# Which units of a transformer layer's second feed-forward product use seven block products, and when their sums are combined

## The chip, the cores and the metric

One core of one Trainium2 chip. The metric is the device time of one execution in microseconds (us), as the median of several runs; single executions that were profiled have a span, from the first to the last instruction, beside it.

## The reference

One decoder layer with 256 tokens of width 1024 in fp32: two groups of attention heads, an output projection, a normalisation, a SwiGLU feed-forward part of inner width 2816, and a second normalisation. The part that the change touches is the last:

```
gu = jnp.einsum('bsd,df->bsf', x, w_ffn_in[l])
g, u = jnp.split(gu, 2, axis=-1)
f = jnp.einsum('bsf,fd->bsd', jax.nn.silu(g) * u, w_ffn_out[l])
x = layer_norm(ALPHA * x + f, ln2_g[l], ln2_b[l])
```

## The kernel before

Every fp32 matrix product is made of three matmuls in a rounded format: an operand is split into a high part (`hi`, a rounding copy on ScalarE) and the rest (`lo`, a subtraction on VectorE), and hi x hi, hi x lo and lo x hi are summed in PSUM. Weights come in units of 128 x 4 x 512 numbers (1 MB). Each is loaded by SyncE's queue into one of the four `raw` buffers of the pool `wraw`, split into one of four `hi` and one of four `lo` buffers, and multiplied.

The inner width 2816 is worked in 11 chunks of 256. The first product (`ffn_rows` for chunks 0 and 1, `ffn_cols` for chunks 2 to 10) needs two weight units per chunk and writes the gated result of chunk c into `hTh[c]` and `hTl[c]`. The second product (from line 650) needs one weight unit per chunk, U0 + v for v = 0 to 10. For a chunk, the output of 256 tokens x 1024 columns is a 2 x 2 matrix of blocks (token tile t of 128, column half n of 512), the inner width gives a 2 x 2 matrix of factors, so a plain unit needs eight block products of three matmuls, 24 in all, which go to the PSUM banks c11, c12, c21 and c22.

For the chunks in `SEVEN` the same blocks come from seven products (Winograd's scheme), 21 matmuls: of the sums T0 to T3 of weight blocks and sums of blocks of h. Products 1, 5, 6 and 7 go to banks of their own and are shared by several output blocks; the other three go to c11, c12 and c21. `ffn_cols` makes the sums of h (lines 615 to 625, tile `hq`), and `split_seven` (line 687) the sums of weights: T in a tile `t` that takes another of the four `raw` buffers, and three of the T split into `th` and `tl` of the pool `tq`, which has two buffers of each. `tq` is opened at line 652, after the pools `hq` and `rpool2` of the first product have been closed at line 646. `load_unit` loads a unit of `SEVEN` in three pieces.

`ahead2(v, 2)` loads up to three units ahead of v and splits up to two ahead. The loop at line 719 multiplies units 0 to 7 (`TAIL` is 8), in the order c11, c12, c21, c22, 1, 6, 5, 7 of each unit. The last three units, 8, 9 and 10, of which 8 and 10 are in `SEVEN`, are multiplied bank by bank from line 735: all three units' products for bank 1, then c11, 6, 5, c12, 7, c22, and behind each of them the operations that add that bank to the output `z` (with alpha times the residual `x1`), each on VectorE but for two copies on ScalarE. The products for c21 come last, in two halves of 256 columns with PSUM tiles of their own (`fo_tail`). `ln_stats` takes the mean and variance (`bn_aggr`, line 510) and a power on GpSimd (line 512); `center` (line 774) and `finish` (line 778) normalise, and each finished piece is stored. The order on each engine is a list that is fixed when the kernel is built; it follows the order in the source where operands are expected to be ready, and takes later work forward where they are not.

Of the kernel before, what the change touches and what calls it, by code (L numbers as in the profile page):

```python
# [11 lines left out]
F32 = mybir.dt.float32  # L12
# [3 lines left out]
ALU = mybir.AluOpType  # L16

P = 128
S = 256
D = 1024  # L20
# [3 lines left out]
NCH = DFF // 256  # L24
# [3 lines left out]
ALPHA = 2.0 ** 0.25  # L28
# [12 lines left out]

SEVEN = (2, 4, 6, 8, 10)


SWAP = [(i + HALF) % 16 if i < 16 else i for i in range(32)]
# [9 lines left out]
def hybrid_layer_kernel(ctx, tc, xT, xr, w_in, w_o, w_f1, w_f2, cols, rows, lamb, rot, tri, out):  # L57
    nc = tc.nc

    const = ctx.enter_context(tc.tile_pool(name="const", bufs=1))  # L60
    wraw = ctx.enter_context(tc.tile_pool(name="wraw", bufs=4))
# [20 lines left out]
    raw, hi, lo = {}, {}, {}  # L82
    state = {"load": 0, "split": 0}

    def load_unit(u, pieces=1):
        t = wraw.tile([P, 4, 512], F32, tag="raw", name=f"raw{u}")
        if u - (NU - NCH) in SEVEN:

            for a, b, w in ((3, 1, 1), (0, 0, 1), (1, 2, 2)):
                nc.sync.dma_start(t[:, a : a + w, :], units[u][:, b : b + w, :])  # L90
            raw[u] = t
            return
        n = 4 // pieces
        for i in range(pieces):
            nc.sync.dma_start(t[:, i * n : (i + 1) * n, :], units[u][:, i * n : (i + 1) * n, :])
        raw[u] = t
# [14 lines left out]
    def split_unit(u, pieces=1):  # L111
        for _ in split_gen(u, pieces):
            pass
# [373 lines left out]
    x1 = lnp.tile([P, 2, D], F32, name="x1")  # L487
    z = mpool.tile([P, 2, D], F32, name="z")
# [8 lines left out]
    st = {}  # L497
# [8 lines left out]
    def ln_stats(name, t):  # L506
        mv = small.tile([P, 2], F32, tag="mv", name=f"mv{name}{t}")
        rs = small.tile([P, 1], F32, tag="rs", name=f"rs{name}{t}")
        n = 4 if (name, t) == ("f", 1) else 2
        nc.vector.bn_aggr(mv, st[name, t][:, :n, :].rearrange("p a b -> p (a b)"))  # L510
        nc.vector.tensor_scalar(rs, mv[:, 1:2], EPS, None, op0=ALU.add)  # L511
        nc.gpsimd.tensor_tensor(rs, rs, mhalf[:, :1], op=ALU.pow)  # L512
        return mv, rs
# [44 lines left out]
    for c in range(NCH):  # L558
        shape = [P, 7, P] if c in SEVEN else [P, 2, S]
        hTh[c] = hp.tile(shape, F32R, name=f"hTh{c}")  # L560
# [33 lines left out]
    def ffn_cols(c, j):  # L594
# [13 lines left out]
        nc.scalar.activation(gate, gate, AF.Silu)  # L608
        if c not in SEVEN:
            nc.vector.tensor_mul(up, up, gate)  # L610
# [40 lines left out]
    TAIL = NCH - 3  # L651
# [5 lines left out]
    bank = {}  # L657
# [6 lines left out]
    def prods(v):  # L664

        u = U0 + v
        H, L = hTh[v], hTl[v]
        W = lambda i: (hi[u][:, i, :], lo[u][:, i, :])
        if v not in SEVEN:
            A = lambda t, kk: (H[:, kk, t * P : (t + 1) * P], L[:, kk, t * P : (t + 1) * P])  # L670
            return {f"c{t + 1}{n + 1}": [(A(t, kk), W(2 * kk + n)) for kk in range(2)]
                    for t in range(2) for n in range(2)}
        A = lambda i: (H[:, i, :], L[:, i, :])
        T = lambda i: (TH[v][:, i, :], TL[v][:, i, :])
        return {"1": [(A(0), W(0))], "c11": [(A(1), W(1))], "6": [(A(5), T(1))], "5": [(A(4), W(3))],
                "c12": [(A(3), W(2))], "7": [(A(6), T(0))], "c21": [(A(2), T(2))]}

    def fo(name, v, last, ps=None, cs=slice(0, 512)):
        todo = prods(v).get(name, ())
        for m, ((ah, al), (wh, wl)) in enumerate(todo):  # L680
            key = name if ps is None else ps.name
            for i, (x, w) in enumerate(((ah, wh), (ah, wl), (al, wh))):
                nc.tensor.matmul(bank[name] if ps is None else ps, x, w[:, cs], start=key not in opened,  # L683
                                 stop=last and (m, i) == (len(todo) - 1, 2))
                opened.add(key)
# [20 lines left out]
    def ahead2(v, splits):  # L706
        u = U0 + v
        while state["load"] <= min(u + 3, NU - 1):
            load_unit(state["load"])
            state["load"] += 1  # L710
        while state["split"] <= min(u + splits, NU - 1):
            n = state["split"]
            state["split"] += 1
            if n - U0 in SEVEN:
                split_seven(n - U0)
            else:
                split_unit(n, 1)

    for v in range(TAIL):
        ahead2(v, 2)  # L720
        for name in ("c11", "c12", "c21", "c22", "1", "6", "5", "7"):
            fo(name, v, (name, v) == ("c21", TAIL - 1))
    ahead2(TAIL, 2)
    tail = range(TAIL, NCH)

    zt = lambda t, n: z[:, t, 512 * n : 512 * n + 512]
    xt = lambda t, n: x1[:, t, 512 * n : 512 * n + 512]
    z = wraw.tile([P, 2, D], F32, tag="raw", name="z2")
    s156 = wraw.tile([P, 3, 512], F32, tag="raw", name="s156")
    s1, s5, s6 = (s156[:, i, :] for i in range(3))  # L730
    st["f", 0] = small.tile([P, 4, 6], F32, tag="st", name="stf0")
    st["f", 1] = small.tile([P, 4, 6], F32, tag="st", name="stf1")

    nc.vector.scalar_tensor_tensor(zt(1, 0), xt(1, 0), ALPHA, bank["c21"], op0=ALU.mult, op1=ALU.add)
    for name in ("1", "c11", "6", "5", "c12", "7", "c22"):
        for v in tail:
            fo(name, v, not any(name in prods(w) for w in tail if w > v))
        if name == "1":
            nc.scalar.copy(s1, bank["1"])
            nc.vector.scalar_tensor_tensor(zt(0, 0), xt(0, 0), ALPHA, s1, op0=ALU.mult, op1=ALU.add)  # L740
        elif name == "c11":
            nc.vector.tensor_add(zt(0, 0), zt(0, 0), bank["c11"])
            nc.vector.bn_stats(st["f", 0][:, 0, :], zt(0, 0))
        elif name == "6":
            nc.vector.tensor_add(s6, s1, bank["6"])
            nc.vector.scalar_tensor_tensor(zt(0, 1), xt(0, 1), ALPHA, s6, op0=ALU.mult, op1=ALU.subtract)
        elif name == "5":
            nc.scalar.copy(s5, bank["5"])
            nc.vector.tensor_add(zt(0, 1), zt(0, 1), s5)
        elif name == "c12":  # L750
            nc.vector.tensor_add(zt(0, 1), zt(0, 1), bank["c12"])
            nc.vector.bn_stats(st["f", 0][:, 1, :], zt(0, 1))
        elif name == "7":
            nc.vector.tensor_add(s6, s6, bank["7"])
            nc.vector.tensor_add(zt(1, 0), zt(1, 0), s6)
            nc.vector.scalar_tensor_tensor(zt(1, 1), xt(1, 1), ALPHA, s6, op0=ALU.mult, op1=ALU.subtract)
            nc.vector.tensor_add(zt(1, 1), zt(1, 1), s5)
        else:
            nc.vector.tensor_add(zt(1, 1), zt(1, 1), bank["c22"])
            for j in range(2):  # L760
                nc.vector.bn_stats(st["f", 1][:, 2 + j, :], z[:, 1, 512 + 256 * j : 768 + 256 * j])

    for t in range(2):
        if t == 1:
            for j in range(2):
                cs, zs = slice(256 * j, 256 * j + 256), slice(256 * j, 256 * j + 256)
                ps = psB.tile([P, 256], F32, tag="b", name=f"fo_tail{j}")
                for v in tail:
                    fo("c21", v, v == NCH - 1, ps, cs)
                nc.vector.tensor_add(z[:, t, zs], z[:, t, zs], ps)  # L770
                nc.vector.bn_stats(st["f", t][:, j, :], z[:, t, zs])
        mv, rs = ln_stats("f", t)
        def center(a, b):
            nc.vector.scalar_tensor_tensor(z[:, t, a:b], z[:, t, a:b], mv[:, 0:1], rows2[:, 0, a:b],
                                           op0=ALU.subtract, op1=ALU.mult)

        def finish(a, b):
            nc.vector.scalar_tensor_tensor(z[:, t, a:b], z[:, t, a:b], rs, rows2[:, 1, a:b], op0=ALU.mult, op1=ALU.add)
            store(a, b)

        def store(a, b):
            nc.sync.dma_start(out[t * P : (t + 1) * P, a:b], z[:, t, a:b])

        if t == 0:
            for n in range(2):
                center(512 * n, 512 * n + 512)
                finish(512 * n, 512 * n + 512)
        else:
            center(512, 1024)
            finish(512, 1024)  # L790
            center(0, 512)
            finish(0, 256)
            finish(256, 512)


# [49 lines left out]
```

## Time and profile before

| | us |
|---|---|
| median of 3 runs | 318.17 |
| lowest and highest run | 318.13, 320.09 |
| profiled execution, its own time | 317.75 |
| its span | 315.8 |
| TensorE busy in the span | 300.4 |
| VectorE busy in the span | 254.3 |
| ScalarE busy in the span | 177.7 |

A profile's timeline gives for each instruction its start in us from the span's start, its length, its engine (PE is TensorE, DVE VectorE, ACT ScalarE, POOL GpSimd, SPq the queue of SyncE), its line, what it writes and reads, and in brackets how long the engine was idle before it and what released it. Consecutive instructions of an engine overlap by some hundredths to a tenth of a us. Matmuls are pipelined: their starts are 0.23 us apart where their lengths read 0.39.

### The profile page before, as it was taken

Reading aid. Unit: us, or ns where it says so; the run is one execution under the profiler, and the core shown is the slowest. Engines: PE = TensorE matmul, PEld = TensorE weight load, DVE = VectorE, ACT = ScalarE, POOL = GpSimd, SP = SyncE. Lnnn points to the kernel's source line nnn. Section 1 sums busy time; section 2 is a strip of 40 time slices with the busy share of each in tenths; the row PEclk is TensorE's granted clock in tenths of the full one; section 3 lists DMA queues with packets and bytes.
Section 4 is the critical chain, followed back from the end, with each engine's and each line's share of the span. In section 5 each row is a group of like instructions: output and inputs, shape, how many; then the busy total and the mean of one; then the engine's idle time right before and its main releaser. Section 6 shows DMA issues by size and latency. Waiting matters only on the chain.

```text
span 315.8 us, 4704 instructions
## 1 busy us (share of the span) xinstructions
PE 300.4 (95%) x1720; PEld 255.6 (81%) x1720; DVE 254.3 (81%) x476; ACT 177.7 (56%) x347; POOL 36.3 (11%) x38
## 2 busy tenths in 40 slices
PE   8899899999999999999999999999999999999960
PEld 5799789867887788888888888888888887888850
DVE  3799999999977289949397598578679779989595
ACT  3857479398685328247377457656664565654000
POOL 1076553310030010100000000000000000000011
PEclk9999999999999999999999999999999999999996
DMA  6989943333376432558654664474362436630002
GB/s 176 391 282 352 413 151 135 133 136 137 141 251 211 195 133 66 222 247 301 230 157 146 230 221 151 162 268 162 126 246 66 175 103 227 236 127 0 0 33 100
DMA packets 13749, 57.17 MB, mean 181 GB/s; under 512 B 1664, under 2 KB 2432, under 8 KB 8864
## 3 DMA queue, kind: packets, MB, share of 16 engines
q1 hardware_dynamic: 13440, 54.79, 49.8%
q0 software_dynamic: 288, 2.10, 1.8%
q8 instruction: 13, 0.21, 0.3%
q14 instruction: 8, 0.07, 0.1%
HBM read 55.84 MB, written 1.05 MB: 180 GB/s over the span
## 4 chain that ended last, share of the span: by engine, by line
PE 74%; DVE 15%; DMA 4%; issue 3%; POOL 1%; ACT 1%; SPq 1%; DVEq 0%; ACTq 0%
PE fc L601 21%; PE foc L683 13%; PE fc L602 11%; DVE lo L108 4%; PE fo L683 4%; DMA raw<-in_w_in_dram 4%; PE wo L142 2%; PE fr L143 2%; PE fr L142 2%; PE wo L144 2%; PE wo L143 2%; PE fr L144 2%; PE pj L142 2%; PE pj L144 2%; PE pj L143 2%
## 5 line engine op out<-in xcount | busy, mean ns | idle before, releaser
L108 DVE TENSOR_TENSOR lo<-raw,hi 128x512 fp32r<-128x512 f32 (+2 forms) x108 | 105.6, 1001 | 20.9 <-ACT hi L106 20.8
L106 ACT CAST hi<-raw 128x512 fp32r<-128x512 f32 (+2 forms) x116 | 90.2, 827 | 22.5 <-PE wo L144 9.9
L601 PE MATMUL fc<-x1T,hi 128*128 128x512 f32 x288 | 100.1, 392 | 0.0
L602 PE MATMUL fc<-x1T,lo 128*128 128x256 f32 x288 | 80.5, 280 | 0.0
L601 PEld LDWEIGHTS fc<-x1T,hi 128*128 128x128 f32 x288 | 54.1, 188 | 11.9
L602 PEld LDWEIGHTS fc<-x1T,lo 128*128 128x128 f32 x288 | 54.0, 188 | 0.0
L142 PE MATMUL pj<-xTh,hi 128*128 128x256 f32 x128 | 36.7, 294 | 1.4 <-ACT hi L190 1.4
L144 PE MATMUL pj<-xTh,lo 128*128 128x256 f32 x128 | 35.7, 286 | 0.6 <-DVE lo L108 0.5
L143 PE MATMUL pj<-xTl,hi 128*128 128x256 f32 x128 | 36.1, 284 | 0.0
L604 ACT COPY v<-fc 128x256 f32<-128x256 f32 x36 | 13.3, 370 | 27.6 <-PE fc L602 27.6
L142 PEld LDWEIGHTS pj<-xTh,hi 128*128 128x128 f32 x128 | 24.3, 192 | 3.0 <-ACT hi L190 2.5
L144 PEld LDWEIGHTS pj<-xTh,lo 128*128 128x128 f32 x128 | 24.1, 191 | 1.3 <-DVE lo L108 0.7
L143 PEld LDWEIGHTS pj<-xTl,hi 128*128 128x128 f32 x128 | 24.5, 191 | 0.0
L605 DVE TENSOR_TENSOR v<-v,fc 128x256 f32<-128x256 f32 x36 | 15.0, 418 | 11.3 <-ACT v L604 11.2
L512 POOL TENSOR_TENSOR rsf<-rsf,mhalf 128x1 f32<-128x1 f32 x2 | 1.8, 922 | 178.6 <-DVE rsf L511 178.6
L683 PE MATMUL foc<-hi,hTl 128*128 128x512 f32 x56 | 22.1, 395 | 0.0
L683 PE MATMUL foc<-lo,hTh 128*128 128x512 f32 x56 | 22.1, 394 | 0.0
L683 PE MATMUL foc<-hi,hTh 128*128 128x512 f32 x56 | 22.1, 394 | 0.0
L108 POOL TENSOR_TENSOR lo<-raw,hi 128x512 fp32r<-128x512 f32 x8 | 13.8, 1723 | 20.1 <-ACT hi L106 20.1
L284 ACT ACTIVATE E<-E,negm 128x128 f32<-128x128 f32 (+1 forms) x32 | 14.2, 444 | 2.5 <-DVE negm L281 2.4
L247 POOL TENSOR_TENSOR sh<-sh,cs_sb 128x256 f32<-128x256 f32 (+1 forms) x12 | 13.3, 1120 | 18.2 <-DVE sh L245 17.5
L142 PE MATMUL pj<-hi,xTh 128*128 128x512 f32 x32 | 13.7, 429 | 0.0
(201 smaller groups left out, 547.5 us busy)
## 6 DMA issues: line engine op xcount, KB each, us to landing
raw<-in_w_f_dram SPq DMA_DIRECT2D x28, 1024.0 KB, 5.1
raw<-in_w_in_dram SPq DMA_DIRECT2D x24, 256.0 KB, 5.5
raw<-in_w_in_dram SPq DMA_DIRECT2D x4, 1024.0 KB, 6.3
raw<-in_w_o_dram SPq DMA_DIRECT2D x4, 1024.0 KB, 4.8
raw<-in_w_f_dram SPq DMA_DIRECT2D x10, 256.0 KB, 3.5
raw<-in_w_f_dram SPq DMA_DIRECT2D x5, 512.0 KB, 4.6
raw<-in_w_in_dram SPq DMA_DIRECT2D x4, 512.0 KB, 8.4
rows<-in_rows_dram POOLq DMA_DIRECT2D x2, 1024.0 KB, 6.6
```

The lines of the kernel that those rows point to most:

```text
L106: nc.scalar.copy(h[:, s, :], r[:, s, :])
L108: eng.tensor_sub(l[:, s, :], r[:, s, :], h[:, s, :].bitcast(F32))
L142: nc.tensor.matmul(ps, sh, mh, start=first, stop=False)
L143: nc.tensor.matmul(ps, sh, ml, start=False, stop=False)
L144: nc.tensor.matmul(ps, sl, mh, start=False, stop=last)
L247: nc.gpsimd.tensor_mul(sh, sh, sin2[:, :m, :])
L284: nc.scalar.activation(e, e, AF.Exp, bias=negm[g][:, i, u : u + 1], scale=-1.0, accum_out=ls[g][:, i, u : u + 1])
L601: nc.tensor.matmul(ps, hi[u][:, i, ws], x1T[:, k], start=k == 0, stop=False)
L602: nc.tensor.matmul(ps[:, 0, :], lo[u][:, i, ws], x1T[:, k, 0, :], start=False, stop=k == KT - 1)
L604: nc.scalar.copy(v, ps[:, 1, :])
L605: nc.vector.tensor_add(v, v, ps[:, 0, :])
L683: nc.tensor.matmul(bank[name] if ps is None else ps, x, w[:, cs], start=key not in opened, stop=last and (m, i) == (len(todo) - 1, 2))
```

## The change

`SEVEN` becomes 2, 3, 4, 6 and 7, so that units 8, 9 and 10 are all plain. Within a unit the order of the products becomes 1, c11, 5, c12, 6, 7, c21, c22. Banks 1, 5, 6 and 7 are complete after unit 7; `combine`, which stands in the source behind all splits and ahead of the last three units' products, adds them and alpha times `x1` into `z`. The last three units then go to c11, c12 and c21, each followed by one sum into `z` and its statistics, and c22 comes last, in two halves of 256 columns. Tile 1 is finished in the order of its columns.

```diff
-SEVEN = (2, 4, 6, 8, 10)
+SEVEN = (2, 3, 4, 6, 7)
...
+    def combine():
+
+        uw = wraw.tile([P, 3, 512], F32, tag="raw", name="uw")
+        nc.scalar.copy(uw[:, 2, :], bank["1"])
+        nc.vector.scalar_tensor_tensor(zt(0, 0), xt(0, 0), ALPHA, bank["1"], op0=ALU.mult, op1=ALU.add)
+        nc.vector.tensor_add(uw[:, 0, :], uw[:, 2, :], bank["6"])
+        for t in range(2):
+            nc.vector.scalar_tensor_tensor(zt(t, 1), xt(t, 1), ALPHA, bank["5"], op0=ALU.mult, op1=ALU.add)
+        nc.vector.tensor_add(uw[:, 1, :], uw[:, 0, :], bank["7"])
+        nc.vector.tensor_sub(z[:, :, 512:], z[:, :, 512:], uw[:, 0:2, :])
+        nc.vector.scalar_tensor_tensor(zt(1, 0), xt(1, 0), ALPHA, uw[:, 1, :], op0=ALU.mult, op1=ALU.add)
+
     for v in range(TAIL):
         ahead2(v, 2)
-        for name in ("c11", "c12", "c21", "c22", "1", "6", "5", "7"):
-            fo(name, v, (name, v) == ("c21", TAIL - 1))
-    ahead2(TAIL, 2)
+        for name in ("1", "c11", "5", "c12", "6", "7", "c21", "c22"):
+            fo(name, v, name in ("1", "5", "6", "7", "c22") and not any(w in SEVEN or name == "c22" for w in range(v + 1, TAIL) if (w in SEVEN) != (name == "c22")))
+    z = wraw.tile([P, 2, D], F32, tag="raw", name="z2")
+    for v in range(TAIL, NCH):
+        ahead2(v, 2)
+    combine()
     tail = range(TAIL, NCH)
...
-    nc.vector.scalar_tensor_tensor(zt(1, 0), xt(1, 0), ALPHA, bank["c21"], op0=ALU.mult, op1=ALU.add)
-    for name in ("1", "c11", "6", "5", "c12", "7", "c22"):
-        for v in tail:
-            fo(name, v, not any(name in prods(w) for w in tail if w > v))
...
+    nc.vector.tensor_add(zt(1, 1), zt(1, 1), bank["c22"])
+    for t in range(2):
+        for n in range(2):
+            name = f"c{t + 1}{n + 1}"
+            if (t, n) != (1, 1):
+                for v in tail:
+                    fo(name, v, v == NCH - 1)
+                nc.vector.tensor_add(zt(t, n), zt(t, n), bank[name])
+                if t == 0:
+                    nc.vector.bn_stats(st["f", 0][:, n, :], zt(0, n))
+                else:
+                    for j in range(2):
+                        nc.vector.bn_stats(st["f", 1][:, j, :], z[:, 1, 256 * j : 256 * j + 256])
+                continue
             for j in range(2):
-                cs, zs = slice(256 * j, 256 * j + 256), slice(256 * j, 256 * j + 256)
+                cs, zs = slice(256 * j, 256 * j + 256), slice(512 + 256 * j, 768 + 256 * j)
                 ps = psB.tile([P, 256], F32, tag="b", name=f"fo_tail{j}")
                 for v in tail:
-                    fo("c21", v, v == NCH - 1, ps, cs)
+                    fo(name, v, v == NCH - 1, ps, cs)
                 nc.vector.tensor_add(z[:, t, zs], z[:, t, zs], ps)
-                nc.vector.bn_stats(st["f", t][:, j, :], z[:, t, zs])
+                nc.vector.bn_stats(st["f", t][:, 2 + j, :], z[:, t, zs])
         mv, rs = ln_stats("f", t)
...
         else:
-            center(512, 1024)
-            finish(512, 1024)
-            center(0, 512)
-            finish(0, 256)
-            finish(256, 512)
+            center(0, 512)
+            finish(0, 512)
+            center(512, 1024)
+            finish(512, 768)
+            finish(768, 1024)
```

## Rows read from the trace of the kernel before

**Rows 1.** The page's part 1: busy us, share of the span, instructions.

```profile
PE 300.4 (95%) x1720; PEld 255.6 (81%) x1720; DVE 254.3 (81%) x476; ACT 177.7 (56%) x347; POOL 36.3 (11%) x38
```

**Rows 2.** Busy time by stretch, with granted clock (PEclk), DMA share, GB/s.

```profile
core 0: us, PE busy (x) PEld busy (x) DVE busy (x) ACT busy (x) POOL busy (x), PEclk, DMA share, GB/s
...
180.00:191.00 11.00, 11.00 (x65) 9.67 (x65) 9.02 (x15) 7.27 (x13) 0.00 (x0) 1.00 0.58 193
247.08:305.20 58.12, 58.12 (x263) 47.28 (x261) 50.81 (x55) 25.83 (x23) 0.93 (x1) 1.00 0.31 109
300.00:316.00 16.00, 5.22 (x35) 4.59 (x33) 12.11 (x26) 0.00 (x0) 1.84 (x2) 0.82 0.18 66
```

**Rows 3.** Timeline of TensorE in the second feed-forward product.

```profile
247.08 0.39 PE L683 MATMUL foc<-hi,hTh 128*128 128x512 f32 x1
...
293.66 0.40 PE L683 MATMUL foc<-hi,hTl 128*128 128x512 f32 x1
...
302.23 0.28 PE L683 MATMUL fo_tail<-th,hTh 128*128 128x256 f32 x1
...
304.94 0.28 PE L683 MATMUL fo_tail<-th,hTl 128*128 128x256 f32 x1
```

**Rows 4.** Chain of waits from 296 on: start us, us, what.

```profile
299.67 0.70 DVE z L751
...
304.44 0.52 issue
304.97 0.68 DVE z L759
...
308.98 0.27 DVE mvf L510
```

**Rows 5.** VectorE by line and form, 240 to 316: busy us, mean ns.

```profile
L108 DVE TENSOR_TENSOR lo<-raw,hi 128x2048 fp32r<-128x2048 f32 x4 | 9.2, 2289 | 2.0 <-ACT hi L106 2.0
L700 DVE TENSOR_TENSOR lo<-raw,hi 128x1536 fp32r<-128x1536 f32 x5 | 8.8, 1754 | 1.9 <-ACT hi L697 1.9
L704 DVE TENSOR_TENSOR tl<-t,th 128x1536 fp32r<-128x1536 f32 x5 | 8.7, 1753 | 0.0
L692 DVE TENSOR_TENSOR t<-raw 128x1024 f32<-128x1024 f32 x5 | 6.1, 1222 | 1.0 <-DMA raw<-in_w_f_dram 1.0
L698 DVE TENSOR_TENSOR t<-t,raw 128x512 f32<-128x512 f32 x5 | 3.4, 690 | 0.0
...
L771 DVE BATCH_NORM_STATS2 stf<-z 128x6 f32<-128x256 f32 x2 | 0.8, 420 | 0.0
```

**Rows 6.** Timeline of ScalarE: the first split that waits for a used-up buffer.

```profile
252.85 1.49 ACT L697 CAST hi<-raw 128x1536 fp32r<-128x1536 f32 x1 [3.00 <-PE foc L683]
```

**Rows 7.** Timelines of VectorE and ScalarE: sums of weights, T parts, tail's start.

```profile
241.64 1.22 DVE L692 TENSOR_TENSOR t<-raw 128x1024 f32<-128x1024 f32 x1
...
257.04 1.09 DVE L570 TENSOR_TENSOR hTl<-hq,hTh 128x896 fp32r<-128x896 f32 x1
...
260.25 2.84 ACT L702 CAST th<-t 128x1536 fp32r<-128x1536 f32 x2
...
262.58 3.42 DVE L704 TENSOR_TENSOR tl<-t,th 128x1536 fp32r<-128x1536 f32 x2
...
290.80 0.68 DVE L734 SCALAR_TENSOR_TENSOR z<-x,foc 128x512 f32<-128x512 f32 x1
```

**Rows 8.** The last load's issue (SyncE's timeline), and loads' median us to landing.

```profile
274.94 1.28 SPq L90 DMA_DIRECT2D raw<-in_w_f_dram  x3
...
raw<-in_w_f_dram SPq DMA_DIRECT2D x28, 1024.0 KB, 5.1
```

**Rows 9.** Timeline of VectorE: bank c11's sum and its statistics.

```profile
294.09 0.69 DVE L742 TENSOR_TENSOR z<-z,foc 128x512 f32<-128x512 f32 x1 [1.44 <-PE foc L683]
294.81 0.69 DVE L743 BATCH_NORM_STATS2 stf<-z 128x6 f32<-128x512 f32 x1
```

More of the change, by code (lines that the diff above doesn't have):

```diff
@@ L717, in ahead2 @@
                 split_unit(n, 1)
+    zt = lambda t, n: z[:, t, 512 * n : 512 * n + 512]
+    xt = lambda t, n: x1[:, t, 512 * n : 512 * n + 512]
+    def combine():
[8 more added lines that the diff above has]
+        nc.vector.scalar_tensor_tensor(zt(1, 0), xt(1, 0), ALPHA, uw[:, 1, :], op0=ALU.mult, op1=ALU.add)
@@ L719, in hybrid_layer_kernel @@
     for v in range(TAIL):
         ahead2(v, 2)
-        for name in ("c11", "c12", "c21", "c22", "1", "6", "5", "7"):
-            fo(name, v, (name, v) == ("c21", TAIL - 1))
-    ahead2(TAIL, 2)
-    tail = range(TAIL, NCH)
[L726 to L730, printed above, removed]
+        for name in ("1", "c11", "5", "c12", "6", "7", "c21", "c22"):
+            fo(name, v, name in ("1", "5", "6", "7", "c22") and not any(w in SEVEN or name == "c22" for w in range(v + 1, TAIL) if (w in SEVEN) != (name == "c22")))
@@ L731, in hybrid_layer_kernel @@
+    z = wraw.tile([P, 2, D], F32, tag="raw", name="z2")
+    for v in range(TAIL, NCH):
+        ahead2(v, 2)
+    combine()
+    tail = range(TAIL, NCH)
     st["f", 0] = small.tile([P, 4, 6], F32, tag="st", name="stf0")
     st["f", 1] = small.tile([P, 4, 6], F32, tag="st", name="stf1")
-    nc.vector.scalar_tensor_tensor(zt(1, 0), xt(1, 0), ALPHA, bank["c21"], op0=ALU.mult, op1=ALU.add)
-    for name in ("1", "c11", "6", "5", "c12", "7", "c22"):
-        for v in tail:
-            fo(name, v, not any(name in prods(w) for w in tail if w > v))
[L738 to L759, printed above, removed]
-            for j in range(2):
-                nc.vector.bn_stats(st["f", 1][:, 2 + j, :], z[:, 1, 512 + 256 * j : 768 + 256 * j])
@@ L763, in hybrid_layer_kernel @@
-    for t in range(2):
-        if t == 1:
-            for j in range(2):
-                cs, zs = slice(256 * j, 256 * j + 256), slice(256 * j, 256 * j + 256)
+    nc.vector.tensor_add(zt(1, 1), zt(1, 1), bank["c22"])
[12 more added lines that the diff above has]
+                continue
+            for j in range(2):
+                cs, zs = slice(256 * j, 256 * j + 256), slice(512 + 256 * j, 768 + 256 * j)
@@ L778, in finish @@
             nc.vector.scalar_tensor_tensor(z[:, t, a:b], z[:, t, a:b], rs, rows2[:, 1, a:b], op0=ALU.mult, op1=ALU.add)
-            store(a, b)
-        def store(a, b):
             nc.sync.dma_start(out[t * P : (t + 1) * P, a:b], z[:, t, a:b])
```

## The prediction

> **What bounds the kernel now.** I read the page's busy shares first: TensorE is busy for 300.4 of the 315.8 us, VectorE for 254.3 [rows 1]. A mean over stages says too little, so next comes the table by stretches. In the second feed-forward product TensorE is busy for all 58.12 us at granted clock 1.00 (its 2.4 GHz level), and VectorE for 50.81; in the last 16 us the roles change, with TensorE at 5.22 and VectorE at 12.11 [rows 2]. So a gain can come from fewer products, which the change doesn't give, or from the end, where TensorE is done and VectorE is not.
>
> The TensorE timeline gives the calendar. The first product of this stage starts at 247.08, the first of half width (256 columns) at 302.23, the last at 304.94, lasting 0.28: the last matmul ends at 305.22 [rows 3]. Between lie 237 full products in 55.15 us, 0.2327 us each, and 23 steps of half width in 2.71 us, 0.118 us each. The chain of waits leaves TensorE at 299.67 and is VectorE's from there to the end; the last `bn_aggr` starts at 308.98 [rows 4]. So 308.98 - 305.22 = 3.76 us after the last matmul VectorE still clears older work: the reader is to see that tile 0's normalisation, the sums of bank 7, s5 and c22 and the last small ones all queue on one engine behind 299.67. From 308.98 to the span's end are 6.8 us of a chain that both kernels have (statistics, the power on GpSimd, two centrings, three finishings, the stores).
>
> **The change, part by part.**
>
> *Products.* A seven-product unit has 21 matmuls, a plain one 24. There are five and six of them before and after: 249 full products' worth. What stands at half width grows from 4 products (24 halves) to 6 (36 halves): 231 x 0.2327 + 36 x 0.118 = 58.0 us against 237 x 0.2327 + 24 x 0.118 = 58.0. From 247.08 that ends at 305.08; the trace had 305.22. Bounds of the difference: -0.14 to 0. I take 305.22.
>
> *Calendar after.* Units 0 to 7 are now three plain and five sevens, 3 x 24 x 0.2327 + 5 x 21 x 0.2327 = 41.2 us, so unit 7 ends near 288.3. Banks c11, c12 and c21 then take 18 products of the last three units each (4.19 us), and close near 292.5, 296.6 and 300.8; the first half of c22 near 303.0, the second at 305.2.
>
> *Splits.* A seven costs VectorE 1.22 + 1.75 + 1.75 and three operations of 0.69 (lines 698, 699 and 703), 6.80 us, a plain unit 2.29 [rows 5], against 4.89 and 5.58 us of products. Three sevens in a row (units 2, 3, 4) leave VectorE 3 x 1.91 = 5.7 us further behind. The cover: the four hi buffers let unit v's split start when unit v-4 is multiplied (unit 4's first copy at 252.85, when unit 0 has just been used up [rows 6]), three units ahead, about 15 us. 15 is over 6.80 + 5.7, so no product starves there; with that cover gone the 5.7 us would stand on TensorE. The total stays five sevens and four plain units from 241.64 on, and VectorE was through with it at 290.80, when the tail's first operation started [rows 7]. After, the seven-product gating of chunk 10, 1.09 us of `hTl` alone [rows 7], is gone from this stretch (it moves to earlier chunks, where VectorE has room: 9.02 busy of 11.00 us where it stood before [rows 2]). Unit 10 is first wanted 12 products behind 288.3, at 291.1. Bounds on its lateness: 290.8 is before 291.1, so 0; from above see the first rival. I take 0, as the T parts come earlier (next) and this unit, now plain, has one `lo` in place of six operations.
>
> *The T parts.* `tq` opens where `hq` and `rpool2` closed. Before, unit 2's th copy ran at 260.25, just behind chunk 10's last store, `hTl` from 257.04 to 258.13, and its tl at 262.58 [rows 7]. After, chunk 10 is plain and the last seven-product chunk is 7, so these parts can come some 7 us earlier (chunk 10's plain `hTl` should end near 251). T work, put last in the new order of names, is wanted at 247.08 + 48 x 0.2327 + 12 x 0.2327 = 261.0 for unit 2. Worth on TensorE: 0 to 0.14 us; I take 0.
>
> *Loads.* Fifteen loads in three pieces per seven stay fifteen; what moves is which. A weight unit and its T sums share four buffers, so loads wait for buffers: the last load was issued at 274.94, lands in about 5.1 us [rows 8], and was wanted over 10 us later. A shift of some 3 us is covered; its cost is 0.
>
> *Combining.* It adds one ScalarE copy and, on VectorE, four `scalar_tensor_tensor`, two sums, one 1024-wide difference and the c22 sum: 4 x 0.68 + 2 x 0.69 + 1.22 + 0.69 = 6.0 us by the nearest rows [rows 5, 7]; a sum out of PSUM costs 0.69 as well [rows 9]. It removes two ScalarE copies and nine 512-wide operations of the old tail that did the same. Bank 1 closes near 284.1 and bank 7 near 287.6, so this lies under the last three units, whose first sum is wanted only at 292.5. Then VectorE has c11's and c12's sums and statistics (2.8), tile 0's statistics, centrings and finishings (3.3), c21 (1.5) and the first half of c22 (0.8): 8.4 us between 292.5 and 305.2. It is idle when the last matmul ends.
>
> *The end.* The c11 row shows the hand-over: the last matmul starts at 293.66 and lasts 0.40, the sum starts at 294.09 [rows 3, 9], 0.03 later; sum to statistics takes 294.81 - 294.09 = 0.72, its length and 0.03. For 256 columns (0.42 each, the sum as the statistics [rows 5]): 305.25, 305.70, `bn_aggr` at 306.15. It was at 308.98. Gain 2.83; with the last matmul at 305.08 it is 2.97, and with the overlap of independent neighbours (0.1 at each of two steps) at most 3.2. I take 2.9.
>
> *Sum.* The profiled execution took 317.75, so 317.75 - 2.9 = 314.85; the median of the runs, 318.17, is 0.42 above it, and 318.17 - 2.9 = 315.27, say 315.3.
>
> **The rivals.**
>
> *The last split queues behind the combining.* VectorE works its list in order: bank c22's last product started before 302.23, but its sum started at 304.97, behind a stretch of 0.52 in which the engine issued nothing [rows 3, 4]. If the combining stands in the list ahead of unit 10's `lo`, that waits for bank 7 (287.6): sum, difference, `scalar_tensor_tensor` and perhaps c22's sum, 0.69 + 1.22 + 0.68 + 0.69 = 3.3, then 2.29: 293.2 against 291.1. TensorE waits 1.4 to 2.1 us; the gain shrinks to 0.8 to 1.5, time 316.7 to 317.4. Against it: unit 10's inputs are ready (hi free at 283.4, copied by 285.4) before most of the banks close. The Trainium skill, "TensorE: Matmul & The Clock Gate", section on architectural detail, says that ScalarE and VectorE are strictly first in, first out; the trace agrees with the c22 row, and by that rule the price above is paid in full if the list has that order.
>
> *Slower: unit 3 has no buffer for its T sums.* If unit 5's load takes the buffer that unit 2's weights leave (the next load took it before), unit 3's sums wait for unit 2's T sums to be split, and with th as late as before (tl from 262.58, two of them to 266.0 [rows 7]) unit 3's four sums start near 264.2. Its last tl would come 1.22 + 2 x 0.69 + 1.42 (th) + 1.75 = 5.8 later, near 270, where TensorE wants it at 265.9: a wait of about 4 us, net +1.2, time 319.4. It decides from the point where that buffer comes free after 263 (a wait over 2.9). Against it: the earlier closing of `hq`.
>
> *Tile 0's normalisation still stands in front of the last sum*, as its centring and finishing did before, from 303 to 307.5. Four operations of 0.65: the gain is 0.3, time 317.9. It would need c12's sum 4 us late.
>
> **How the numbers follow.** Forecast 0.64, queued split 0.17, slower rival 0.11, tile 0 in front 0.08. The predicted time is the forecast's, 315.3; its own range is 314.5 (gain 3.2, less the 0.42 between profiled run and median) to 315.8. The range that should hold 8 in 10 reaches over the first and third rivals to 318.0. A measurement of this kernel can tell about 1%, 3.2 us, from no change. The forecast's 2.9 is 0.91%: just inside. Some 0.27 of the chance lies beyond 3.2 us. Slower by over 1% needs a wait of over 6 us, the slower rival gone worse: 0.05. The rest, 0.68, is within 1%.
>
> **What would show it.** Right: TensorE's products run from about 247.1 to 305.2 at 0.233 us with no hole, VectorE is idle when the last matmul ends, the last `bn_aggr` starts 0.9 us later, and the span is near 312.9. The first rival shows as a hole of TensorE near 291 ended by `lo`, the second as holes at 264 to 270 ended by th or tl, the third as centrings between the last matmul and its sum. The prediction is wrong if the stage's start moves from 247.1, or if `bn_aggr` still starts 3 us or more behind the last matmul.

## The result, and the profile after

The changed kernel takes 314.69 us in the median of four runs (314.48 to 314.95), the kernel before 318.21 beside it (four runs, 318.13 to 320.09): a ratio of 0.9884, with a 95% interval of 0.9856 to 0.9913. The profiled execution took 314.95, with a span of 313.2; that of before took 317.75, with 315.8. The time lies in the predicted range, 0.6 below the predicted 315.3. It is 1.2% faster. The likeliest of the prediction's three cases was a change within 1%; the measured value lies beyond that, and its interval reaches to both sides (0.9% to 1.4%).

The page's busy shares differ from [rows 1] by almost nothing:

```profile
PE 300.7 (96%) x1726; PEld 256.2 (82%) x1726; DVE 254.3 (81%) x475; ACT 177.6 (57%) x346; POOL 36.3 (12%) x38
```

VectorE works as long as before, 254.3 us, and TensorE 0.3 us longer. So no busy time was saved; work was moved. The same table by stretches as [rows 2] says where (columns as there):

```profile
core 0: us, PE busy (x) PEld busy (x) DVE busy (x) ACT busy (x) POOL busy (x), PEclk, DMA share, GB/s
...
247.08:305.20 58.12, 58.12 (x270) 47.78 (x269) 52.40 (x57) 25.30 (x22) 0.93 (x1) 1.00 0.34 118
300.00:316.00 16.00, 5.45 (x42) 5.01 (x40) 7.76 (x17) 0.00 (x0) 0.92 (x1) 0.76 0.18 66
```

VectorE's 12.11 us in the last 16 have become 7.76, and in the stage it is busy for 52.40 instead of 50.81. TensorE fills the stage in both kernels at granted clock 1.00. Its timeline answers [rows 3]; the first product, the first half product and the last one are

```profile
247.37 0.39 PE L683 MATMUL foc<-hi,hTh 128*128 128x512 f32 x1
...
301.02 0.28 PE L683 MATMUL fo_tail<-hi,hTh 128*128 128x256 f32 x1
...
305.17 0.28 PE L683 MATMUL fo_tail<-hi,hTl 128*128 128x256 f32 x1
```

From the first start to the last end that is 305.45 - 247.37 = 58.08 us; before it was 305.22 - 247.08 = 58.14. No hole lies between. The chain of waits (start us, us, what) is the counterpart of [rows 4]:

```profile
288.37 12.82 PE foc L683 x55
301.18 4.28 PE fo_tail L683 x36
305.46 0.03 issue
305.48 0.43 DVE z L766
305.92 0.02 issue
305.94 0.44 DVE stf L767
306.38 0.02 issue
306.40 0.28 DVE mvf L510
```

In [rows 4] the chain left TensorE at 299.67 and was VectorE's for nine us before `bn_aggr`. Now it stays on TensorE until the last matmul, and only three VectorE operations follow, with 0.02 to 0.03 us of issue between them. From the last matmul's end to `bn_aggr` are 0.95 us, where there were 3.76. Counted from the start of the stage, `bn_aggr` comes after 306.40 - 247.37 = 59.03 us, before after 308.98 - 247.08 = 61.90: a gain of 2.87 us. VectorE's timeline shows what stands where now:

```profile
287.97 2.29 DVE L108 TENSOR_TENSOR lo<-raw,hi 128x2048 fp32r<-128x2048 f32 x1 [0.85 <-ACT hi L106]
290.18 0.68 DVE L726 SCALAR_TENSOR_TENSOR z<-x,fo 128x512 f32<-128x512 f32 x1
...
295.50 0.68 DVE L747 TENSOR_TENSOR z<-z,foc 128x512 f32<-128x512 f32 x1
...
297.02 0.69 DVE L754 TENSOR_TENSOR z<-z,foc 128x512 f32<-128x512 f32 x1 [0.24 <-PE foc L683]
...
298.79 1.40 DVE L771 SCALAR_TENSOR_TENSOR z<-z,mvf,rows 128x512 f32<-128x512 f32 x2
300.11 1.41 DVE L775 SCALAR_TENSOR_TENSOR z<-z,rsf,rows 128x512 f32<-128x512 f32 x2
...
305.48 0.42 DVE L766 TENSOR_TENSOR z<-z,fo_tail 128x256 f32<-128x256 f32 x1 [1.25 <-PE fo_tail L683]
305.94 0.43 DVE L767 BATCH_NORM_STATS2 stf<-z 128x6 f32<-128x256 f32 x1
306.40 0.27 DVE L510 BATCH_NORM_AGGREGATE mvf<-stf 128x2 f32<-128x24 f32 x1
```

Unit 10's `lo`, at 287.97, is the last split. The combining follows it, from 290.18 to 296.18 with c11's sum among it, tile 0's normalisation is over at 301.52, and ahead of the last sum VectorE has been idle for 1.25 us, waiting for TensorE.

### The profile page after: what moved, and what is told of

Its sections match the earlier page's. It is cut to its first block, busy times and chain, and to the rows that moved or that the text cites. A ratio compares the mean times of both kernels' runs of the same rounds, so it can differ in the third digit from the quotient of the medians.

```text
span 313.2 us, 4707 instructions
## 1 busy us (share of the span) xinstructions
PE 300.7 (96%) x1726; PEld 256.2 (82%) x1726; DVE 254.3 (81%) x475; ACT 177.6 (57%) x346; POOL 36.3 (12%) x38
## 4 chain that ended last, share of the span: by engine, by line
PE 76%; DVE 12%; DMA 4%; issue 3%; POOL 1%; ACT 1%; SPq 1%; DVEq 0%; ACTq 0%
PE fc L601 21%; PE foc L683 13%; PE fc L602 11%; PE fo L683 4%; DVE lo L108 4%; DMA raw<-in_w_in_dram 4%; PE wo L142 3%; PE fr L143 2%; PE fr L142 2%; PE wo L144 2%; PE wo L143 2%; PE fr L144 2%; PE pj L142 2%; PE pj L144 2%; PE pj L143 2%
## 5 line engine op out<-in xcount | busy, mean ns | idle before, releaser
L683 PE MATMUL foc<-lo,hTh 128*128 128x512 f32 x52 | 20.5, 395 | 0.0
L683 PE MATMUL foc<-hi,hTl 128*128 128x512 f32 x52 | 20.5, 394 | 0.0
L683 PE MATMUL foc<-hi,hTh 128*128 128x512 f32 x52 | 20.5, 394 | 0.0
```

## The experiments

Ratios are to the kernel before, on the same chip. Where a few tenths of a us count, the text compares the time from the stage's first product to the last `bn_aggr`: the stage's start differs by 0.6 us between executions of one kernel (247.37, 247.21 and 246.76 in three profiles of the changed kernel), and by more between kernels. The changed kernel ran on one chip with the next three kernels below, and on another with the last two; for the rest, a comparison with it is one between chips.

**The changed kernel again.** No edit, two more times, each beside other kernels.

> The changed kernel once more, as the mark for the runs beside it. Backlog theory (the gain is VectorE work that used to be left behind the last matmul): 314.5 to 315.0 us, TensorE without a hole from about 247.4 to 305.5, the last bn_aggr 0.9 to 1.0 us behind the last matmul's end.

Median 314.75, ratio 0.9889 [0.9859, 0.9919]. From the stage's start `bn_aggr` comes after 59.00 us.

> The changed kernel once more, as the mark for the two runs beside it: 314.5 to 315.0 us.

Median 315.03, ratio 0.9911 [0.9883, 0.9938]; 59.04 us. So the 59.03 is steady to some hundredths, and three medians lie between 314.69 and 315.03: the gain is 3.0 to 3.5 us in the medians.

**The set of units alone.** The kernel before, with the new `SEVEN` and nothing else but the places at which the shared banks close. Their sums, the order of the products within a unit and c21 as the last bank stay as they were.

```diff
-SEVEN = (2, 4, 6, 8, 10)
+SEVEN = (2, 3, 4, 6, 7)
...
-            fo(name, v, (name, v) == ("c21", TAIL - 1))
+            fo(name, v, v == TAIL - 1 and name in ("c21", "1", "6", "5", "7"))
```

> Only SEVEN becomes 2, 3, 4, 6, 7; the old order of products, the old sums of the banks and c21 last stay, and banks 1, 5, 6 and 7 are closed after unit 7. Backlog theory: the sums of the four shared banks have their inputs by 288 and get taken forward under the last three units, so VectorE is idle at the last matmul and the time is that of the changed kernel within 0.3 us, 314.5 to 315.1. Rival (the gain needs the rewritten sums, fewer operations and c22 last): a good part of the old 3.8 us behind the last matmul is left, 316 to 317.5. Rival (it needs the new order of products): 316 or more, with holes of TensorE before th or tl.

Median 315.16, ratio 0.9901 [0.987, 0.9932]; from the stage's start 58.98 us. In VectorE's timeline the last sum waits for TensorE as in the changed kernel:

```profile
305.32 0.42 DVE L770 TENSOR_TENSOR z<-z,fo_tail 128x256 f32<-128x256 f32 x1 [1.25 <-PE fo_tail L683]
```

The whole gain up to `bn_aggr` comes with the set. The new `combine` with its alpha x1, the new order of names and c22 as the last bank add nothing to it that the profile shows. The medians of this kernel and of the changed one on the same chip (315.16 and 314.75) are 0.4 us apart, which is within both intervals. About 0.1 of it stands behind `bn_aggr`: from there to the end of the span are 6.85 us here, as in the kernel before, and 6.75 in the changed kernel. What the rest is stays open.

**The old order of products within a unit.**

```diff
-        for name in ("1", "c11", "5", "c12", "6", "7", "c21", "c22"):
+        for name in ("c11", "c12", "c21", "c22", "1", "6", "5", "7"):
```

> The changed kernel with the old order of products within a unit (c11, c12, c21, c22, 1, 6, 5, 7). Backlog theory: the same time as the changed kernel within 0.3 us, since the T parts come early enough for either order and the banks close under 4 us later with over 8 us of cover. Rival (the order keeps TensorE from waiting for the T parts): holes ended by th or tl at units 2 to 7, 0.5 to 3 us slower, 315.2 to 317.7.

Median 315.3, ratio 0.99 [0.986, 0.994]; 58.99 us from the stage's start (which came at 247.75), and TensorE has no hole. The median is 0.55 us above the changed kernel's beside it, just inside the range of the expectation's rival; but the rival's sign, holes ended by `th` or `tl`, isn't there, and up to `bn_aggr` the stage takes as long as in the changed kernel. So no worth of the order shows here: T parts come early enough for either.

**Shared banks closed late.** The changed kernel, with unit 7's products for banks 1, 5, 6 and 7 behind the last three units' products for c11, c12 and c21. The same products in all, the same operations on VectorE; only the combining can't begin before the end of the stage.

```diff
         for name in ("1", "c11", "5", "c12", "6", "7", "c21", "c22"):
+            if v == TAIL - 1 and name in ("1", "5", "6", "7"):
+                continue
...
-    combine()
     tail = range(TAIL, NCH)
+    for name in ("c11", "c12", "c21"):
+        for v in tail:
+            fo(name, v, v == NCH - 1)
+    for name in ("1", "5", "6", "7"):
+        fo(name, TAIL - 1, True)
+    combine()
```

> The changed kernel, but unit 7's products for banks 1, 5, 6 and 7 are issued behind the last three units' products for c11, c12 and c21, so that the four shared banks close about 12 us later, with the same products and the same VectorE operations. Backlog theory: VectorE gets 13 us of sums, statistics and tile 0's normalisation from about 299 on, the last bn_aggr comes near 312 in place of 306.4, and the time is 319.5 to 321. Rival (the end is not set by VectorE's queue but by matmuls, the power on GpSimd and the stores): 314.5 to 315.5.

Median 322.64, ratio 1.0147 [1.0104, 1.0189]: slower than the changed kernel by 8 us and than the kernel before by 4.5. VectorE's timeline (first row and last) shows its work in one piece:

```profile
299.98 0.69 DVE L726 SCALAR_TENSOR_TENSOR z<-x,fo 128x512 f32<-128x512 f32 x1 [10.31 <-ACT uw L725]
...
313.16 0.26 DVE L510 BATCH_NORM_AGGREGATE mvf<-stf 128x2 f32<-128x24 f32 x1
```

It was idle for 10.31 us and then busy for 13.2 without a pause up to `bn_aggr`. TensorE's one long wait stands in its own timeline:

```profile
301.02 0.39 PE L683 MATMUL fo<-th,hTl 128*128 128x512 f32 x1
303.71 0.39 PE L683 MATMUL fo_tail<-hi,hTh 128*128 128x256 f32 x1 [2.30 <-DVE z L759]
```

The half product for c22 starts 2.69 us after the product before it, where 0.23 is normal: it is released by bank c11's sum (line 759 in this kernel, 302.98 to 303.66), which stands behind the combining. From 305.04 to 308.45 the granted clock is then 0.50, the 1.2 GHz level; TensorE is done at 309.76 even so, before VectorE reaches the last sums at 311.72. So the gain depends on the place in time at which the shared banks close, as the theory has it. That the last units of the new set have lighter splits accounts for half a us at most: VectorE was through with its splits at 290.80 before and at 290.26 after. The size was underestimated: the profiled execution lies 0.7 us and the median 1.6 above the expected range. VectorE's 13.2 us were as expected, but they started about 1 us later than thought, behind ScalarE's copy of bank 1.

**Five sevens in a row.** Does the cover of about 15 us in the prediction's split step hold where two more units' splits fall behind?

```diff
-SEVEN = (2, 3, 4, 6, 7)
+SEVEN = (3, 4, 5, 6, 7)
```

> SEVEN is 3, 4, 5, 6, 7: five sevens in a row in place of three, the same products and operations in all. By the prediction's own step (units are split three units, about 15 us, ahead, and each seven in a row puts VectorE 1.9 us behind) 6.8 + 5 x 1.9 = 16.3 us is more than the cover: a hole of TensorE of 1 to 2 us, 315.7 to 316.7. Rival (the cover is in the total, not in the row, so any order does): 314.5 to 315.1. Rival (loads are the bound, since weights and T sums share four buffers): holes near units 8 to 10 of 2 us and more, ended by a copy that waited for a load, 316.7 or more.

Median 315.16, ratio 0.9904 [0.9874, 0.9934]; 59.30 us from the stage's start, 0.3 more than the changed kernel. (The stage starts at 249.75 in this profile; of the 2.4 us more than in the changed kernel's, 2.0 are there by 18 us, behind a stretch at granted clock 0.50 from 11.8 to 15.2.) One hole of some 0.4 us stands at 293.5 to 294.4. It is not one of a split that starves in the row: it is the last plain unit's, whose copy on ScalarE waits for its load.

```profile
289.74 1.91 ACT L106 CAST hi<-raw 128x2048 fp32r<-128x2048 f32 x1 [1.44 <-DMA raw<-in_w_f_dram]
```

Its `lo` ended at 293.97 on VectorE, and TensorE waited for it. The load had been issued at 282.6, as soon as VectorE's last sum of weights (line 699) let its buffer go, and landed at 289.71. So VectorE's lateness reaches TensorE by way of a buffer and a load, as the expectation's second rival had it, at a fifth of that rival's price. The expected hole of 1 to 2 us didn't come: five sevens in a row put VectorE further behind than three do, and no product of the row itself starves.

**Four and six sevens.** A seven has three matmuls fewer than a plain unit, 3 x 0.2327 = 0.70 us. If TensorE sets the end, that is the price of a unit each way.

```diff
-SEVEN = (2, 3, 4, 6, 7)
+SEVEN = (2, 3, 4, 6)
```

> SEVEN is 2, 3, 4, 6, four sevens. TensorE has three matmuls more, 0.7 us; VectorE has 4.5 us less. Backlog theory (VectorE is off the path in the changed kernel, TensorE sets the end): 0.7 us slower than the changed kernel, 315.2 to 315.7. Rival (VectorE's splits still cost TensorE something in the changed kernel): the same or faster than it, 313.5 to 314.8.

Median 315.87, ratio 0.9918 [0.9887, 0.9948]; 59.77 us from the stage's start, 0.73 to 0.77 more than the changed kernel. The median is 0.2 above the expected range. VectorE has less to do here, and the stage grows by just the three matmuls: TensorE sets the end.

```diff
-SEVEN = (2, 3, 4, 6, 7)
+SEVEN = (2, 3, 4, 5, 6, 7)
...
-    hq = f1x.enter_context(tc.tile_pool(name="hq", bufs=2))
+    hq = f1x.enter_context(tc.tile_pool(name="hq", bufs=1))
```

> SEVEN is 2 to 7, six sevens, and the tile hq has one buffer in place of two to make room. TensorE has three matmuls less, 0.7 us; VectorE has 4.5 us more of splits. If VectorE's splits in this stage have under 1 us of room at unit 10, as the changed kernel's trace reads (its last lo ends 0.8 us before it is wanted), but 3.4 us of idle before that: a hole of 1 to 2 us, 315.0 to 316.3. Rival (the splits have the room that the cover of 15 us says): 0.7 us faster than the changed kernel, 313.8 to 314.3.

> Six sevens (2 to 7, one hq buffer) once more, with more rounds. If what its first trace showed holds (no hole of TensorE, the last matmul 0.7 us earlier from the stage's start, bn_aggr 1.17 us behind it), it is 0.2 to 0.5 us faster than the changed kernel: 314.2 to 314.6. If the late last split does cost TensorE a hole in some executions: 314.8 to 316.

Medians 314.52 and 314.35, ratios 0.989 [0.9845, 0.9935] and 0.9866 [0.9828, 0.9904]. The hole that the first expectation gave doesn't come. Products take 57.34 us from first start to last end where the changed kernel's take 58.08: the 0.7 is there. But `bn_aggr` comes after 58.50 and 58.51 us, only 0.5 earlier. VectorE's timeline of the second of the two:

```profile
303.36 0.74 DVE L775 SCALAR_TENSOR_TENSOR z<-z,rsf,rows 128x512 f32<-128x512 f32 x1
304.02 0.74 DVE L759 BATCH_NORM_STATS2 stf<-z 128x6 f32<-128x256 f32 x2
304.69 0.73 DVE L766 TENSOR_TENSOR z<-z,fo_tail 128x256 f32<-128x256 f32 x2
305.34 0.74 DVE L767 BATCH_NORM_STATS2 stf<-z 128x6 f32<-128x256 f32 x2
306.11 0.26 DVE L510 BATCH_NORM_AGGREGATE mvf<-stf 128x2 f32<-128x24 f32 x1
```

No row has an idle time before it: both halves of c22 are added in one go, and `bn_aggr` starts 1.17 us behind the last matmul instead of 0.95. VectorE is last again, by 0.2 us, and a seventh seven would gain little more this way. This is the fastest version, by 0.2 to 0.7 us in medians, which is less than the intervals tell apart; counted from the stage's start in the profiles, by 0.5.

**The last split's `lo` three times.** The prediction's first rival let `lo` of unit 10 come 2 us late and charged it to TensorE in full. Here that subtraction is computed three times over, 4.58 us more on VectorE; nothing else changes.

```diff
-            eng.tensor_sub(l[:, s, :], r[:, s, :], h[:, s, :].bitcast(F32))
+            for _ in range(3 if u == NU - 1 else 1):
+                eng.tensor_sub(l[:, s, :], r[:, s, :], h[:, s, :].bitcast(F32))
```

> The changed kernel, but unit 10's lo is computed three times over, 4.4 us more of VectorE in front of its first use. If the room there is 0.8 us, as the changed kernel's trace reads, TensorE gets a hole of about 3.3 us near 291, and the time is 317.5 to 318.5. Rival (room of several us, as the prediction's calendar of loads had it): 314.5 to 315.5.

Median 316.25, ratio 0.9936 [0.9917, 0.9954]; `bn_aggr` 59.90 us after the stage's start, 0.9 later than in the changed kernel. (The median is 1.2 to 1.6 us above the changed kernel's; what it has beyond the 0.9 is open.) The time lies between the two expected ranges. The expected hole of 3.3 us isn't there: the last matmul ends at 305.23. The list was made with the longer split in it, and puts other products ahead of those that need unit 10's `lo`: c11's sum comes only at 296.57 instead of 293.17, and TensorE has no gap. The 0.9 stands at the end, in VectorE's timeline:

```profile
292.34 2.29 DVE L109 TENSOR_TENSOR lo<-raw,hi 128x2048 fp32r<-128x2048 f32 x1
...
305.64 0.74 DVE L767 TENSOR_TENSOR z<-z,fo_tail 128x256 f32<-128x256 f32 x2
306.30 0.74 DVE L768 BATCH_NORM_STATS2 stf<-z 128x6 f32<-128x256 f32 x2
307.08 0.26 DVE L511 BATCH_NORM_AGGREGATE mvf<-stf 128x2 f32<-128x24 f32 x1
```

The third `lo` ends at 294.63, three and a half us behind the 291.1 at which the prediction wanted it, and TensorE doesn't wait. Of 4.58 us added, 0.9 arrive: VectorE had some 3.7 us of room under the last three units. That room, not a split's due time, is the margin of this change for work that is in the list. A lateness that comes in the run, as the load's with five sevens in a row, did cost TensorE 0.4 us.

**A smaller last step.** c22's last 256 columns as two pieces of 128, with eight pieces of statistics, to leave less behind the last matmul.

```diff
-    st["f", 1] = small.tile([P, 4, 6], F32, tag="st", name="stf1")
+    st["f", 1] = const.tile([P, 8, 6], F32, name="stf1")
...
-            for j in range(2):
-                cs, zs = slice(256 * j, 256 * j + 256), slice(512 + 256 * j, 768 + 256 * j)
-                ps = psB.tile([P, 256], F32, tag="b", name=f"fo_tail{j}")
+            for j, (a, b) in enumerate(((0, 256), (256, 384), (384, 512))):
+                cs, zs = slice(a, b), slice(512 + a, 512 + b)
+                ps = psB.tile([P, b - a], F32, tag="b", name=f"fo_tail{j}")
```

> The changed kernel with the last 256 columns of c22 in two pieces of 128 columns, and tile 1's statistics in eight pieces of 128. VectorE's sum and statistics behind the last matmul shrink from 0.43 + 0.44 to about 0.29 + 0.29. If the matmuls of 128 columns take a quarter of 0.233 us (0.06), the last bn_aggr comes 0.3 us earlier: 314.2 to 314.6. Rival (a matmul of 128 columns takes as long as one of 256, 0.118, as its weights must be loaded too): 18 x 0.06 = 1.1 us later, net 0.8 slower: 315.3 to 315.8.

Median 318.96, ratio 1.0012 [0.9986, 1.0037]: the gain is gone. TensorE's timeline shows one reason:

```profile
305.50 0.28 PE L683 MATMUL fo_tail<-hi,hTl 128*128 128x128 f32 x1
305.61 0.28 PE L683 MATMUL fo_tail<-hi,hTh 128*128 128x128 f32 x1
```

Matmuls of 128 columns start 0.112 us apart, those of 256 columns 0.118. The 36 small ones take 4.0 us where 18 of 256 columns took 2.1: 1.9 us more. A hole of 0.3 us at 289.4 comes on top, and 0.27 us of shorter operations behind the last matmul come off (0.69 us to `bn_aggr` instead of 0.95). So `bn_aggr` comes 60.94 us after the stage's start, 1.9 later than in the changed kernel. The expectation had charged the small ones 0.06 each; its rival had their time nearly right (0.118), but counted 18 of them instead of 36.

A second loss, of 1.8 us, lies ahead of the stage, which starts at 249.21. It is no wait. In the first feed-forward product (read from 165 to 240 us), matmuls of 512 columns start 0.235 us apart in the mean where the changed kernel's start 0.229 apart, at granted clock 1.00 in both, and this adds up to 1.7 us by the stage's start. The edit touches nothing there but the pool of one small tile; why these matmuls slow down is open.

**Six sevens, with one of the sums of weights on GpSimd.** Since VectorE was last again with six, the sum of line 699 (six times 0.69 us) goes to an engine that is nearly idle in this stage.

```diff
-SEVEN = (2, 3, 4, 6, 7)
+SEVEN = (2, 3, 4, 5, 6, 7)
...
-        nc.vector.tensor_add(t[:, 3, :], t[:, 2, :], r[:, 1, :])
+        nc.gpsimd.tensor_add(t[:, 3, :], t[:, 2, :], r[:, 1, :])
```

(with `hq` in one buffer, as above)

> Six sevens (2 to 7, one hq buffer), and the fourth weight sum of each seven on GpSimd in place of VectorE, which takes 6 x 0.6 = 3.6 us off VectorE. With six sevens alone TensorE ended 0.4 to 0.6 us earlier than in the changed kernel, with no hole, but VectorE was still busy then, and the last bn_aggr came 1.17 us behind the last matmul in place of 0.95. With VectorE relieved bn_aggr comes 0.95 behind it again: 0.2 us faster than six sevens alone, 314.0 to 314.4. Rival (GpSimd's sums of 1.7 us hold back the last T parts, or slow VectorE beside them): a hole of TensorE ended by th or tl, 314.8 or more.

Median 323.99, ratio 1.0147 [1.0092, 1.0203]: 9.5 us slower in the medians than six sevens without it. The expectation's rival came. Three views show why: first the table of instructions for GpSimd (240 to 316: busy us, mean ns, idle before), then the waits (us in total, times, longest), then the table by stretches with the columns as above:

```profile
L699 POOL TENSOR_TENSOR t<-t,raw 128x512 f32<-128x512 f32 x6 | 13.1, 2191 | 147.6 <-DVE t L698 140.4 <-ACT hi L697 7.2
```

```profile
ACT th L702 <- POOL t L699: 15.3, 5, 4.0
...
DVE tl L704 <- ACT th L702: 6.4, 3, 2.7
PEld fo L683 <- DVE tl L704: 4.9, 4, 1.6
...
PEld fo L683 <- DVE lo L703: 3.1, 2, 1.9
```

```profile
280.00:288.00 8.00, 5.47 (x23) 3.89 (x22) 7.01 (x5) 3.89 (x3) 2.09 (x1) 1.00 0.36 136
288.00:292.50 4.50, 2.57 (x10) 1.44 (x9) 1.93 (x3) 1.40 (x2) 1.53 (x1) 1.00 0.85 324
292.50:299.50 7.00, 5.78 (x13) 4.22 (x14) 6.78 (x5) 4.16 (x4) 0.00 (x0) 0.52 0.08 33
```

The sum takes 2.19 us in the mean on GpSimd, against 0.69 on VectorE. ScalarE's `th` waits for it, VectorE's `tl` for that, and TensorE for `tl` (PEld is its loading of weights). Twice TensorE waits for the `lo` of line 703, which VectorE itself runs more slowly beside a sum on GpSimd (see the last section). TensorE, which fills this stage in most of the other kernels, is busy for 5.47 us of 8.00 and 2.57 of 4.50. Then its granted clock falls to 0.52 in the mean of the stretch, that is the 1.2 GHz level for nearly all of it, and 13 matmuls stand in 5.78 busy us; their starts are 0.43 apart instead of 0.233. The stage's products take 68.3 us instead of 57.3: some 8.5 us are holes, some 2.5 us the lower clock. A transfer of VectorE's work onto a longer chain of three engines has cost more than the work.

## Why the prediction was right, step by step

**What bounds the kernel**: as read. One row was misread. The 0.52 us of "issue" ahead of c22's sum [rows 4] are not a stretch in which VectorE issued nothing; its timeline of before has a finishing operation of tile 0 there, up to the sum's start at 304.97:

```profile
304.30 0.74 DVE L778 SCALAR_TENSOR_TENSOR z<-z,rsf,rows 128x512 f32<-128x512 f32 x1
```

So VectorE was busy there too, and the backlog is the one that the prediction counted. This backlog behind the last matmul was the only thing that the change could win, and 2.81 of the 3.76 us between the last matmul and `bn_aggr` went. With late banks the backlog comes back and is worse.

**Products and calendar**: 58.08 us measured, 58.0 worked out. The first half product was put near 300.8 and started at 301.02, where the stage had started 0.3 later. By the letter of the prediction a moved start of the stage is a sign of its being wrong; with 247.37, 247.21 and 246.76 in three profiles, 0.3 us is the spread of executions.

**Splits**: no hole, as forecast. The cover of some 15 us was enough, even for five sevens in a row, but for the 0.4 us that a late load cost there. The lateness of unit 10 was taken as 0 because its split would end at 290.8 or before; it ended at 290.26. But the deadline of 291.1 behind that wasn't one: with `lo` at 294.63 no product waited, as the list of products had been made for it.

**T parts**: the forecast was 7 us earlier; unit 2's `tl` moved from 262.58 [rows 7] to 254.25, 8.3 us. TensorE got at most 0.1 us from it: before, unit 2's first two products with `th` start 0.34 us apart (261.76 and 262.10) instead of 0.23, the only such gap in the stage.

**Loads**: undersized, without consequence. The last load was issued at about 279.7 instead of 274.94 [rows 8], a shift of 5 us where the prediction said 3. It waited for the buffer that VectorE's `lo` of another unit set free at 279.66, so VectorE's pace reaches the loads too. The copies of units 9 and 10 wait for their loads, in ScalarE's timeline:

```profile
281.21 1.91 ACT L106 CAST hi<-raw 128x2048 fp32r<-128x2048 f32 x1 [3.09 <-DMA raw<-in_w_f_dram]
...
286.02 1.91 ACT L106 CAST hi<-raw 128x2048 fp32r<-128x2048 f32 x1 [0.94 <-DMA raw<-in_w_f_dram]
```

Unit 10's load landed at 285.94, and "wanted over 10 us later" was too generous: ScalarE stood ready for its copy 0.94 us before. "Copied by 285.4" in the first rival was 2.5 us early, so that `lo`, at 290.26, was only 0.8 us ahead of the planned 291.1. That this cost nothing was in part luck: with five sevens in a row the same load lands later, and TensorE waits.

**Combining**: 6.0 us forecast for eight operations. They stand between 290.18 and 296.18, 6.0 us, with c11's sum taken in among them (their neighbours overlap a little). They replace ten operations of 512 columns in the old tail, not nine; no term of the sum hangs on that. c11's sum was wanted at 292.5 and came at 293.17, behind most of the combining; that cost nothing, since 1.25 us of idle time were left before the last sum.

**The end**: `bn_aggr` 0.95 us behind the last matmul, forecast 0.93; gain 2.87, forecast 2.83 to 2.97.

**The rivals**: none came. The queued split had `lo` (287.97) ahead of all combining in VectorE's list. The missing buffer would have shown at 264 to 270, where TensorE has no hole. Tile 0's normalisation ran from 298.79 to 301.52, four us ahead of the last sum. The first rival's price was wrong: with the triple `lo` the split ended 4.4 us later (294.63 instead of 290.26), which cost TensorE nothing and the end 0.9 us, where the rival charged 1.4 to 2.1 us for less. What failed is the step from a late operand to a waiting TensorE, since the products behind could be exchanged when the list was made. The rule that the prediction set beside it (the Trainium skill, "TensorE: Matmul & The Clock Gate", architectural detail: ScalarE and VectorE first in, first out) isn't touched by that. The row of c22 agrees with it (its last product starts before 302.23, its sum at 304.97, behind other work), and no run here tests it further.

**The number**: the sum went from profile to profile and then added the 0.42 us by which the median of before lay above its profile. From profile to profile the gain is 2.80 us: the 2.87, less 0.29 by which the stage starts later, and 0.2 more behind `bn_aggr` and outside the span. For the changed kernel the median lies 0.26 below its profile (314.69, 314.95), and in its two repeats 0.01 below and 0.70 above. As far as the runs show, that is the spread of single executions. It makes 3.5 us between the medians out of 2.80 between the profiles, so the 0.6 us by which the time lies below the forecast are no term of the sum. The interval of 0.9856 to 0.9913, 2.8 to 4.6 us, holds both. With a forecast at 0.91% and such a spread, 0.68 for "within 1%" and 0.27 for "over 1%" leaned too far to one side: 0.09% of the time, 0.3 us, lay between the forecast and the bound.

## What to carry to other kernels

Where an engine has a backlog behind the last matmul, first count what in it can start earlier, and change which operands close early: here a different choice of units moved three us of VectorE work without shortening its busy time. Judge the move by the room that is left on that engine under the last stage (3.7 us here), not by the due time of one operand, as far as the order of the products can be made for it; a load that comes later than planned still holds TensorE up. And stop when both engines end together: with six units VectorE was last again, and only 0.5 of 0.7 us arrived.

## What the runs showed of the hardware

A matmul of 128 columns is hardly cheaper than one of 256 (0.112 and 0.118 us from start to start), while one of 512 takes 0.233, all at granted clock 1.00 and each with a load of 128 x 128 weights of its own. What sets the 0.112 no run separates. A smaller last step pays on VectorE (0.29 us for 128 columns of sum, 0.42 for 256) and not on TensorE.

A 128 x 512 sum on GpSimd took between 1.29 and 4.87 us beside a busy VectorE, and VectorE's operations beside it became longer: its `lo` from a sum (line 703) went from 689 ns in the mean, in the changed kernel, to 1007, and `lo` of three parts (line 700) from 1755 to 1934. The timelines of the two engines show one of them waiting for the other:

```profile
265.45 1.29 POOL L699 TENSOR_TENSOR t<-t,raw 128x512 f32<-128x512 f32 x1 [7.20 <-ACT hi L697]
...
265.75 1.55 DVE L703 TENSOR_TENSOR lo<-t,hi 128x512 fp32r<-128x512 f32 x1 [0.79 <-ACT hi L701]
```

VectorE's `lo` starts beside GpSimd's sum and ends at 267.30, 0.56 us behind the sum's end at 266.74; alone it takes 0.69. The other way round, the sum of 4.87 us began at 253.38, while VectorE worked from 253.08 to 257.09, and ended 1.2 us behind that. The Trainium skill, "SBUF — State Buffer", section "SBUF: two separate sides", says that GpSimd and a VectorE operation with two operands in SBUF share one pair of ports, which one of them holds for a whole instruction while the other waits; both stretched sides agree with that.

Holes of 0.5 to 1.6 us from 271 on, in that kernel, were followed by nearly seven us at granted clock 0.50, from 292.75 to 299.58. With late banks one hole of 2.5 us (products start at 301.02 and next at 303.71) was followed by 3.4 us at 0.50, from 305.04 to 308.45; matmuls of 256 columns started 0.213 us apart in it instead of 0.118. The clock was at 1.00 again behind both.
